# One hybrid layer in f32: where the sums of weight blocks for the up projection are made, and when those for the other products run

## The chip, the cores and the metric

The kernel is one program on one core of a Trainium2 chip. The metric is the device time of one execution in microseconds. A core has TensorE (PE; its weight loads are listed apart as PEld), VectorE (DVE), ScalarE (ACT), GpSimd (POOL) and SyncE (SP), and 16 DMA engines that serve all queues. Here SP issues the loads of weights, and POOL issues small stores and the block sums described below.

## The reference

One layer of a decoder trunk, sequence and width 1024, all of it f32. `u` is the modulated input:

```python
mod = cond @ w_ada[l] + b_ada[l]
shift1, scale1, gate1, shift2, scale2, gate2 = jnp.split(mod[:, None, :], 6, axis=-1)
u = x * (1.0 + scale1) + shift1
hq, hf, hi, hg, rq, rk, rv, rg, ga, gb = jnp.split(u @ w_in[l], split_at, axis=-1)
ya = _hgrn2(hq, hf, hi, hg, lower_bounds[l]) @ w_pa[l]
yb = _retention(rq, rk, rv, rg, positions) @ w_pb[l]
y = (jax.nn.sigmoid(ga) * ya + jax.nn.sigmoid(gb) * yb) @ w_o[l]
x = _layer_norm(DEEPNORM_ALPHA * x + (1.0 + gate1) * y, ln1_g[l], ln1_b[l])
u = x * (1.0 + scale2) + shift2
h = jnp.square(jax.nn.relu(u @ w_up[l] + b_up[l]))
y = h @ w_down[l] + b_down[l]
x = _layer_norm(DEEPNORM_ALPHA * x + (1.0 + gate2) * y, ln2_g[l], ln2_b[l])
```

`w_in` has the columns of HGRN2 (`hq` to `hg`, 8 heads of 128), of retention (`rq` to `rg`, 4 heads) and of the two gates (`ga`, `gb`, 1024 each). `w_pb` is 2048x1024, `w_up` 1024x4096, `w_down` 4096x1024.

## The kernel before

**Products.** Every f32 product is made of three matmuls on halves: `split` writes a rounded copy `hi` (ACT, L181) and the rest `lo` (DVE, L182), and `mm3` multiplies hi by hi, hi by lo and lo by hi (L186 to L188). A `mm3` of 512 columns is three matmuls of 128x512.

**Block products.** The six large products (`gb`, `rg`, `pa`, `pb`, `up`, `dn`) cut both factors into 2x2 blocks and use a scheme of seven block products, q1 to q7, in place of eight. Some take a sum of weight blocks for their weights: with w11, w12, w21, w22 as the blocks, q5 needs s1 = w21 + w22, q6 s2 = s1 + w11, q3 s4 = s2 + w12 and q7 s3 = w11 + w21 (the signs are put into the activations). The activations have such variants too; `t_sums` makes them on DVE, once for each large product.

**The sums.** Each large product is cut into parts (gb 2, rg 4, pa 2, pb 4, up 8, dn 8). `block_sums` makes a part's four sums in DRAM, on POOL's DMA queue: four copies (L207) and four accumulating DMAs (L208) of 512 KB each, 224 DMAs for all 28 parts. `start_sums` puts them in one list behind the start of the program, in the order of the products that need them, and `mm3` takes one from it whenever 14*512 matmul columns have gone by: every fifth `mm3` of 512 columns. `after` ties each to that `mm3`'s last matmul, so that POOL issues it then and not before.

**The stream of weights.** `build_stream` lists every weight tile in the order of use. SP loads pieces of 512 KB into `raw` (three buffers, `_load`), `_split_to` makes `wh` and `wl` of them (three buffers each), two tiles ahead of the product that uses them. Pieces of `w_ada` go through the same `raw` buffers: DVE reads them directly in `ada_step` (L376 and L378, results in `acc`) during retention, four groups of two pieces for each head.

**Order of the program.** The start (to about 60 us); HGRN2, with the projection for `ga` at its end (to about 660); retention, four heads (`r_head`, to 1180; `t` at L762 is the rotation, `gl` and `knl` are halves made by `split`); the gates (`GATE_STEPS`, from 1180); the merge of the branches (to about 1650), the output projection and its norm (`out_proj`, 1650 to 1743; `rs` at L1253 is a row's inverse deviation, made on POOL, `z_d` a store); up (`ffn_up`, 1743 to 2046); down (`ffn_down`, to the end). A scheduler orders each engine's instructions within this.

**Up.** `UP_STEPS` runs q1 and q2 of parts 0 and 1, then q5, q6, q7, q3, q4 of part 0, the same of part 1, and then parts 2 to 7, each in the order q1, q5, q6, q2, q7, q3, q4. A step is 24 matmuls of 128x512. In the first steps DVE and ACT also make the four variants of the activations. `up_block` (L1357 in the trace) writes the squared ReLU into `hv` (two buffers); `part_sums` (L957 to L960) and `last_sum` (L963 to L965) add up its variants for down on DVE and store them to `hv_d` by POOL's queue, one pair of groups after the other. Banks of PE's results are called `psa` to `psd`; `group_out` copies a finished one to `o` (L992).

Of the kernel before, what the change touches and what calls it, by code (L numbers as in the profile page):

```python
# [9 lines left out]
F32 = mybir.dt.float32  # L10
# [4 lines left out]
ALU = mybir.AluOpType  # L15
# [3 lines left out]
P = 128  # L19
# [42 lines left out]
DN_ORDER = ("q1", "q5", "q6", "q3", "q7", "q2", "q4")  # L62
SECOND = ("q2", "q5", "q3")


def group_steps(parts):

    a = parts[:2]
    return ([(q, *x) for q in ("q1", "q2") for x in a] + [(q, *x) for x in a for q in UP_ORDER if q not in ("q1", "q2")] +
            [(q, *x) for x in parts[2:] for q in UP_ORDER])  # L70
# [2 lines left out]
GATE_STEPS = group_steps([("gb", p) for p in range(2)] + [("rg", p) for p in range(4)])  # L73
UP_STEPS = group_steps([("up", p) for p in range(8)])
LAST = 4
PREP = 14 * 512

H_DEFER = (3, 8)
H_ORDER = (("hq", "hf", "hg", "hi"), ("hg", "hi", "hq", "hf"))
# [48 lines left out]
class Rows:  # L128


    def __init__(self, pool):
        self.pool = pool
# [15 lines left out]
class Trunk:  # L148
    def __init__(self, ctx, tc, ins, out):
        self.ctx, self.tc, self.nc, self.i, self.out = ctx, tc, tc.nc, ins, out  # L150
        self.n = 0
        self.pend = []
        self.prep = []
        self.cols_done = 0
        self.paced = False

    def later(self, steps, fn):
        self.pend.append([steps, fn])
# [25 lines left out]
    def mm3(self, out, wh, wl, uh, ul, start, stop, more=False):  # L184
        mm = self.nc.tensor.matmul
        r = mm(out, wh, uh, start=start, stop=False, skip_group_check=more)  # L186
        mm(out, wh, ul, start=False, stop=False, skip_group_check=more)  # L187
        l = mm(out, wl, uh, start=False, stop=stop, skip_group_check=more)  # L188
        self.cols_done += 3 * out.shape[-1]
        if self.paced and self.cols_done >= PREP:  # L190
            self.cols_done = 0
            if self.prep:
                self.after(self.prep.pop(0)(), l)
        return r, l
# [22 lines left out]
            add(3, s4[p], s2[p])  # L217
        return {"q1": w11, "q2": w12, "q3": s4, "q4": w22, "q5": s1, "q6": s2, "q7": s3}

    def start_sums(self):  # L220

        late = lambda n: n // 8 + self.sums[n][0]
        self.prep = [self.sums[n][1] for n in sorted(range(len(self.sums)), key=lambda n: (late(n), n))]
        self.paced = True

    def after(self, a, b):

# [16 lines left out]
    def spec_N(self, w, r0, c0, key):  # L244
# [2 lines left out]
        tiles = [(key + (i,), [((lambda d: d.rearrange("p (k c) -> p k c", k=4)), i, (lambda a: a))]) for i in (0, 1)]  # L247
        return pcs, tiles

    def spec_1(self, ap, key):  # L250
        return [ap], [(key, [((lambda d, a=ap: d if len(a.shape) == 2 else d.rearrange("p (k c) -> p k c", k=a.shape[1])), 0, (lambda a: a))])]

    def build_stream(self, specs):
        self.w_tiles = []
        self.w_pcs = []
        for pcs, tiles in specs:
            base = len(self.w_pcs)
            self.w_pcs += pcs
            for key, ops in tiles:
                self.w_tiles.append((key, [(d, base + i, s) for d, i, s in ops]))  # L260
        self.w_raw = {}
        self.w_dst = {}
        self.w_done = {}
        self.w_next = self.w_split = self.w_load = 0
# [13 lines left out]
    def _split_to(self, n):  # L278
        while self.w_split < min(n, len(self.w_tiles)):
            key, ops = self.w_tiles[self.w_split]  # L280
            self._load_to(max(i for _, i, _ in ops) + 3)
            if key[0] == "ada":
                self.w_done[self.w_split] = [self.w_raw[i] for _, i, _ in ops]
                self.w_split += 1
                continue
            if key[0] == "wo":
                self.split(self.woh[key[1]], self.wol[key[1]], self.w_raw[ops[0][1]])
                self.w_done[self.w_split] = None
                self.w_split += 1
                continue  # L290
            if key in self.w_dst:
                hi, lo = self.w_dst[key]
            else:
                hi = self.wp.tile([P, 1024], F32R, tag="wh", bufs=3, name=self.uid("wh"))
                lo = self.wp.tile([P, 1024], F32R, tag="wl", bufs=3, name=self.uid("wl"))
            for d, i, s in ops:
                self.split(d(hi), d(lo), s(self.w_raw[i]))
            self.w_done[self.w_split] = (hi, lo)
            self.w_split += 1
# [1138 lines left out]
def build(ctx, tc, ins, out):  # L1438
    k = Trunk(ctx, tc, ins, out)
# [25 lines left out]
    specs = []  # L1465
# [6 lines left out]
    for h in range(RH):  # L1472
        specs.append(k.spec_T(w_in, 0, C_RQ + 256 * h, ("rq", h), inter=True))
        specs.append(k.spec_T(w_in, 0, C_RK + 256 * h, ("rk", h), inter=True))
        for b in (0, 1):
            specs.append(k.spec_N(w_in, 0, C_RV + 512 * h + 256 * b, ("rv", h, b)))
            for s, g in ADA_ORDER[4 * h + 2 * b:4 * h + 2 * b + 2]:
                c0 = s * D + 256 * g
                pcs = [ins["w_ada"][512 * i:512 * i + 512, c0:c0 + 256].rearrange("(k p) c -> p k c", p=P) for i in (0, 1)]
# [1 line left out]
    k.sums = []  # L1481
    wv = {}
    for name, w, cut, n in (("gb", w_in[:, C_GB:C_GB + 1024], 1, 2), ("rg", w_in[:, C_RG:C_RG + 2048], 1, 4),
                            ("pa", ins["w_pa"], 0, 2), ("pb", ins["w_pb"], 0, 4),
                            ("up", ins["w_up"], 1, 8), ("dn", ins["w_down"], 0, 8)):
        wv[name] = k.block_sums(name, w, cut, n)
    parts = lambda q, name, p: k.spec_1(wv[name][q][p].rearrange("(k p) c -> p k c", p=P), (q, name, p))
    specs += [parts(*x) for x in GATE_STEPS]
    specs += [parts(q, "pa", p) for q in MERGE_ORDER for p in range(2)]
    for n, (q, p) in enumerate((q, p) for q in MERGE_ORDER for p in range(4)):  # L1490
        specs.append(parts(q, "pb", p))
        if n % 3 == 2 and n // 3 < KT:
            specs.append(k.spec_1(ins["w_o"][n // 3 * P:(n // 3 + 1) * P, :], ("wo", n // 3)))
    specs += [parts(*x) for x in UP_STEPS]
    specs += [parts(q, "dn", p) for q in DN_ORDER for p in range(8)]
    k.build_stream(specs)
    upool, u12pool = ExitStack(), ExitStack()
# [2 lines left out]
    with ExitStack() as s:  # L1500
        k.st = k.pool("start", "right", s)
        k.start()
    k.start_sums()
    k.hst = {}
    k.rot = k.rotary()
    with ExitStack() as s:
# [20 lines left out]
    late, fo = k.gates(rs.close, u12pool.close)  # L1527
# [13 lines left out]
    k.u2f = {}  # L1541
    ops = ExitStack()
    k.op = k.pool("op", "right", ops)
    k.out_proj()

    def close():
# [37 lines left out]
```

## Time and profile before

| | before |
|---|---|
| median of 3 runs (lowest, highest) | 2366.46 us (2359.39, 2379.37) |
| the profiled execution | 2367.19 us, span 2365.4 us |
| granted clock of PE, mean | 0.993 |
| busy: PE, PEld | 2302.0 us (97%), 1970.3 us (83%) |
| busy: DVE, ACT, POOL | 1496.8 us (63%), 911.4 us (39%), 362.8 us (15%) |
| POOL's DMA queue (software) | 213.42 MB, 33.9% of the 16 engines' span |
| SP's DMA queue (hardware) | 245.04 MB, 31.7% |

The span runs from the first to the last recorded instruction; the execution's own time holds a little more. A row of an engine's timeline reads: start, length, engine, line, operation, result <- operands, shape, the number of instructions taken together, and in square brackets the idle time ahead of it with what ended that. A row of the waits reads: who waited <- for whom: total us, how many times, the longest.

### The profile page before, as it was taken

Reading aid. Unit: us, or ns where it says so; the run is one execution under the profiler, and the core shown is the slowest. Engines: PE = TensorE matmul, PEld = TensorE weight load, DVE = VectorE, ACT = ScalarE, POOL = GpSimd, SP = SyncE. Lnnn points to the kernel's source line nnn. Section 1 sums busy time; section 2 is a strip of 40 time slices with the busy share of each in tenths; the row PEclk is TensorE's granted clock in tenths of the full one; section 3 lists DMA queues with packets and bytes.
Section 4 is the critical chain, followed back from the end, with each engine's and each line's share of the span. In section 5 each row is a group of like instructions: output and inputs, shape, how many; then the busy total and the mean of one; then the engine's idle time right before and its main releaser. Section 6 shows DMA issues by size and latency. Waiting matters only on the chain.

```text
span 2365.4 us, 31820 instructions
## 1 busy us (share of the span) xinstructions
PE 2302.0 (97%) x12146; PEld 1970.3 (83%) x12146; DVE 1496.8 (63%) x2684; ACT 911.4 (39%) x1425; POOL 362.8 (15%) x543
## 2 busy tenths in 40 slices
PE   7999999999999999999989999999999999999998
PEld 5888888988779898998978887888888888888886
DVE  7886756577274746556485676667786444544578
ACT  4522222221223232433454444453456555544332
POOL 0222221222312222221232211000000000000000
PEclk9999999999999999999999999999999999999999
DMA  9757565656884967758667867776226464865674
GB/s 268 188 148 163 145 149 152 150 135 161 229 225 107 226 174 175 209 140 228 137 207 246 289 231 277 267 262 231 85 99 218 165 222 161 311 219 190 210 239 155
DMA packets 260361, 460.94 MB, mean 195 GB/s; under 512 B 15488, under 2 KB 158064, under 8 KB 253552
## 3 DMA queue, kind: packets, MB, share of 16 engines
q0 software_dynamic: 65600, 213.42, 33.9%
q1 hardware_dynamic: 194288, 245.04, 31.7%
q8 instruction: 95, 1.56, 0.3%
q14 instruction: 58, 0.48, 0.1%
q10 hardware_dynamic: 320, 0.45, 0.1%
HBM read 380.20 MB, written 196.09 MB: 244 GB/s over the span
## 4 chain that ended last, share of the span: by engine, by line
PE 87%; DVE 7%; DMA 4%; issue 1%; POOL 1%; ACT 1%; ACTq 0%; DVEq 0%; SPq 0%; POOLq 0%
PE psd L188 17%; PE psd L187 17%; PE psd L186 17%; PE psc L186 4%; PE psc L188 4%; PE psc L187 4%; PE psa L188 3%; PE psa L187 3%; PE psa L186 3%; PE psa L590 3%; PE psb L866 3%; DMA raw<-in_w_ada 3%; PE psc L853 2%; PE psb L186 1%; PE psb L187 1%; PE psb L188 1%
## 5 line engine op out<-in xcount | busy, mean ns | idle before, releaser
L182 DVE TENSOR_TENSOR wl<-raw,wh 128x1024 fp32r<-128x1024 f32 (+1 forms) x312 | 328.1, 1057 | 276.4 <-ACT wh L181 272.1
L181 ACT ACTIVATE wh<-raw 128x1024 fp32r<-128x1024 f32 (+1 forms) x312 | 287.8, 929 | 442.0 <-PE psd L187 239.8
L186 PE MATMUL psd<-uh,wh 128*128 128x512 f32 x788 | 315.9, 402 | 0.0
L187 PE MATMUL psd<-ul,wh 128*128 128x512 f32 x788 | 314.2, 399 | 0.4 <-DVE ul L182 0.4
L188 PE MATMUL psd<-uh,wl 128*128 128x512 f32 x788 | 314.2, 399 | 0.0
L186 PE MATMUL psd<-wh,uh 128*128 128x256 f32 x768 | 221.0, 288 | 0.0
L187 PE MATMUL psd<-wl,uh 128*128 128x256 f32 x768 | 218.3, 284 | 0.0
L188 PE MATMUL psd<-wh,ul 128*128 128x256 f32 x768 | 218.1, 284 | 0.0
L182 DVE TENSOR_TENSOR hl<-hr,hh 128x1024 fp32r<-128x1024 f32 x96 | 117.1, 1221 | 132.8 <-ACT hh L181 132.8
L187 PEld LDWEIGHTS psd<-ul,wh 128*128 128x128 f32 x788 | 149.5, 190 | 28.8 <-DVE ul L182 1.2
L188 PEld LDWEIGHTS psd<-uh,wl 128*128 128x128 f32 x788 | 149.4, 190 | 28.5
L186 PEld LDWEIGHTS psd<-uh,wh 128*128 128x128 f32 x788 | 149.1, 190 | 28.3 <-ACT uh L181 0.7
L181 ACT ACTIVATE hh<-hr 128x1024 fp32r<-128x1024 f32 x96 | 101.4, 1056 | 178.9 <-PE psb L187 68.1
L186 PEld LDWEIGHTS psd<-wh,uh 128*128 128x128 f32 x768 | 147.0, 191 | 2.9 <-issue 2.6
L187 PEld LDWEIGHTS psd<-wl,uh 128*128 128x128 f32 x768 | 147.0, 191 | 0.4
L188 PEld LDWEIGHTS psd<-wh,ul 128*128 128x128 f32 x768 | 147.1, 191 | 0.0
L597 DVE COPY_PREDICATED hS<-mask,psa 128x128 f32<-128x128 uint8 x288 | 77.2, 314 | 28.5 <-PE psa L590 25.9
L823 DVE SCALAR_TENSOR_TENSOR vl<-psd,cst,vh 128x256 fp32r<-128x256 f32 x64 | 30.8, 482 | 76.0 <-ACT vh L822 76.0
L822 ACT ACTIVATE vh<-psd,cst 128x256 fp32r<-128x256 f32 x64 | 30.3, 474 | 117.0 <-PE psd L188 114.6
L590 PE MATMUL psa<-qp,k 128*128 128x192 f32 x384 | 72.6, 329 | 1.3 <-DVE k L566 1.3
L590 PEld LDWEIGHTS psa<-qp,k 128*128 128x128 f32 x384 | 62.1, 189 | 10.4 <-issue 5.0
L1253 POOL TENSOR_TENSOR rs<-rs,mhalf 128x1 f32<-128x1 f32 x16 | 12.0, 747 | 369.9 <-DVE rs L1252 340.5
(503 smaller groups left out, 5687.2 us busy)
## 6 DMA issues: line engine op xcount, KB each, us to landing
raw<-in_w_in SPq DMA_DIRECT2D x90, 512.0 KB, 5.2
hr<-hv_d SPq DMA_DIRECT2D x56, 512.0 KB, 3.5
up_s<-in_w_up POOLq DMA_DIRECT2D x48, 512.0 KB, 5.8
dn_s<-in_w_down POOLq DMA_DIRECT2D x48, 512.0 KB, 5.4
hv_d<-hv POOLq DMA_DIRECT2D x16, 1280.0 KB, 5.8
raw<-in_w_ada SPq DMA_DIRECT2D x32, 512.0 KB, 6.5
raw<-up_s SPq DMA_DIRECT2D x32, 512.0 KB, 6.0
raw<-dn_s SPq DMA_DIRECT2D x32, 512.0 KB, 4.4
```

What stands on the lines that cost most here:

```text
L181: self.nc.scalar.activation(hi, src, AF.Copy)
L182: self.nc.vector.tensor_tensor(lo, src, hi.bitcast(F32), op=ALU.subtract)
L186: r = mm(out, wh, uh, start=start, stop=False, skip_group_check=more)
L187: mm(out, wh, ul, start=False, stop=False, skip_group_check=more)
L188: l = mm(out, wl, uh, start=False, stop=stop, skip_group_check=more)
L590: nc.tensor.matmul(pa[:, c * 192:(c + 1) * 192].rearrange("p (b w r) -> p b w r", w=2, r=3 * sz), k[:, n * P:(n + 1) * P], mv, start=True, ...
L597: V.copy_predicated(dst, self.mask8[:, o:o + 128].rearrange("p (b two s) -> p b two s", two=2, s=sz), src)
L822: nc.scalar.activation(hi, pd, AF.Copy, scale=sc)
L823: nc.vector.scalar_tensor_tensor(lo, pd, sc, hi.bitcast(F32), op0=ALU.mult, op1=ALU.subtract)
L853: mm(G[e], l[:, n % 2, es], r, start=n == 0 and i == 0, stop=i == 2, skip_group_check=n > 0)
L866: mm(po, l, r, start=i == 0, stop=i == len(pairs) - 1)
L1253: nc.gpsimd.tensor_tensor(rs, rs, self.mhalf[:, :1], op=ALU.pow)
```

## The change

Three things change.

1. Up's 64 sums in DRAM go. Its stream holds the blocks of `w_up` themselves (`spec_sums`), and `sum_split` adds them in SBUF on DVE just ahead of the split. q5 loads w21 and w22 and writes their sum into two new tiles `ws` of 128x512; q6 adds w11 to them, and q2's block w12 is added behind its own split, so that q3 finds its weights in `ws`. Parts 0 and 1 run q2 first, so there q3 loads w12 again. q7 loads w11 and w21 and adds them in place. q5, q6 and q3 are split in halves.
2. The rest of the list is cut in two. The 96 sums of `gb`, `rg`, `pa` and `pb` start behind the start as before; the 64 of `dn` start at the output projection.
3. `PREP` goes from 14*512 to 17*512: one sum for every sixth `mm3` of 512 columns in place of every fifth.

```diff
+BLOCKS_OF = {"q1": [(0, 0)], "q2": [(0, 1)], "q3": [], "q4": [(1, 1)], "q5": [(1, 0), (1, 1)], "q6": [(0, 0)], "q7": [(0, 0), (1, 0)]}
...
-PREP = 14 * 512
+PREP = 17 * 512
...
-        if self.paced and self.cols_done >= PREP:
+        if self.cols_done >= PREP:
...
-    def start_sums(self):
-
-        late = lambda n: n // 8 + self.sums[n][0]
-        self.prep = [self.sums[n][1] for n in sorted(range(len(self.sums)), key=lambda n: (late(n), n))]
-        self.paced = True
+    def start_sums(self, n):
+
+        now, self.sums = self.sums[:n], self.sums[n:]
+        late = lambda n: n // 8 + now[n][0]
+        self.prep += [now[n][1] for n in sorted(range(len(now)), key=lambda n: (late(n), n))]
+        self.cols_done = 0
...
+    def spec_sums(self, w, steps):
+
+        kh, nh = w.shape[0] // 2, w.shape[1] // 2
+        specs, seen = [], set()
+        for q, name, p in steps:
+            late = q == "q3" and (name, p, "q2", "early") in seen
+            if q == "q2" and (name, p, "q6") not in seen:
+                seen.add((name, p, "q2", "early"))
+            seen.add((name, p, q))
+            need = [(0, 1)] if late else BLOCKS_OF[q]
+            pcs = [w[kh * k:kh * k + kh, nh * m + 256 * p:nh * m + 256 * p + 256].rearrange("(k p) c -> p k c", p=P) for m, k in need]
+            specs.append((pcs, [((q, name, p), [(None, i, late) for i in range(len(pcs))])]))
+        return specs
+
+    def sum_split(self, q, hi, lo, raws, late):
+
+        V = self.nc.vector
+        hi, lo = (x.rearrange("p (k c) -> p k c", k=4) for x in (hi, lo))
+        if q in ("q5", "q6", "q3"):
+            if q == "q5":
+                self.ws = [self.gp.tile([P, 2, 256], F32, tag="gate", bufs=2, name=self.uid("ws")) for _ in (0, 1)]
+            for k, s in zip((slice(0, 2), slice(2, 4)), self.ws):
+                if q == "q5":
+                    V.tensor_tensor(s, raws[0][:, k], raws[1][:, k], op=ALU.add)
+                elif q == "q6" or late:
+                    V.tensor_tensor(s, s, raws[0][:, k], op=ALU.add)
+                self.split(hi[:, k], lo[:, k], s)
+            return
+        if q == "q7":
+            V.tensor_tensor(raws[0], raws[0], raws[1], op=ALU.add)
+        self.split(hi, lo, raws[0])
+        if q == "q2" and self.ws_open:
+            for k, s in zip((slice(0, 2), slice(2, 4)), self.ws):
+                V.tensor_tensor(s, s, raws[0][:, k], op=ALU.add)
...
-                            ("pa", ins["w_pa"], 0, 2), ("pb", ins["w_pb"], 0, 4),
-                            ("up", ins["w_up"], 1, 8), ("dn", ins["w_down"], 0, 8)):
+                            ("pa", ins["w_pa"], 0, 2), ("pb", ins["w_pb"], 0, 4), ("dn", ins["w_down"], 0, 8)):
...
-    specs += [parts(*x) for x in UP_STEPS]
+    specs += k.spec_sums(ins["w_up"], UP_STEPS)
...
-    k.start_sums()
+    k.start_sums(96)
...
+    assert not k.prep
+    k.start_sums(64)
     k.out_proj()
```

**POOL's queue in retention.** Before, the list runs through retention; `small` (L883) is a head norm's inverse deviation, and the DMAs between are copies for up's sums:

```order
L883 TENSOR_TENSOR small_6836<-small_6836,mhalf 128x1
L207 DMA up_s_6_185<-in_w_up 512x256
L883 TENSOR_TENSOR small_6897<-small_6897,mhalf 128x1
L883 TENSOR_TENSOR small_6977<-small_6977,mhalf 128x1
L207 DMA up_s_6_193<-in_w_up 512x256
L883 TENSOR_TENSOR small_7038<-small_7038,mhalf 128x1
L207 DMA up_s_6_201<-in_w_up 512x256
L883 TENSOR_TENSOR small_7114<-small_7114,mhalf 128x1
L207 DMA up_s_6_209<-in_w_up 512x256
```

In the changed kernel the last sums of the first list (`pb`) stand among the last stores of `ga`, which end HGRN2, and the first norms of retention (now L928) follow with no sum between them:

```order
L719 DMA ga_d_87<-gate_5699 128x512
L209 DMA pb_s_3_170<-pb_s_3_166 64x2048
L209 DMA pb_s_3_178<-pb_s_3_170 64x2048
L719 DMA ga_d_87<-gate_5729 128x512
L719 DMA ga_d_88<-gate_5763 128x512
L719 DMA ga_d_88<-gate_5791 128x512
L958 DMA g_d_130<-brow_6543 16x1x16
L958 DMA g_d_130<-brow_6658 16x1x16
L928 TENSOR_TENSOR small_6760<-small_6760,mhalf 128x1
L928 TENSOR_TENSOR small_6820<-small_6820,mhalf 128x1
```

The sums have left retention's rows of POOL; the norms follow one another there.

**POOL's queue at the end of the output projection and in up.** Before, the stores of `hv_d` for the first pair of groups come right behind the projection's own work:

```order
L1253 TENSOR_TENSOR rs_15957<-rs_15957,mhalf 128x1
L1339 DMA z_d_112<-rows1l 128x1024
L960 DMA hv_d_119<-hv_16291 128x2560
L960 DMA hv_d_119<-hv_16309 128x2560
L965 DMA hv_d_119<-hv_16291 128x1024
L965 DMA hv_d_119<-hv_16309 128x1024
```

In the changed kernel down's sums (copies L208, accumulating DMAs L209) stand around the same stores (now L1005 and L1010):

```order
L208 DMA dn_s_4_183<-in_w_down 256x512
L208 DMA dn_s_4_191<-in_w_down 256x512
L208 DMA dn_s_4_199<-in_w_down 256x512
L208 DMA dn_s_4_207<-in_w_down 256x512
L1005 DMA hv_d_119<-hv_16180 128x2560
L1005 DMA hv_d_119<-hv_16198 128x2560
L1010 DMA hv_d_119<-hv_16180 128x1024
L1010 DMA hv_d_119<-hv_16198 128x1024
L209 DMA dn_s_2_205<-dn_s_2_189 64x2048
L209 DMA dn_s_3_190<-dn_s_3_182 64x2048
```

Each sum waits for its `mm3`, and a store behind it in the queue waits with it.

**ACT's queue where part 0 of up hands over to part 1.** Before, the first two writes of `hv` (L1357) stand ahead of the copies of the banks `psd` and `psb` (L992):

```order
L992 ACTIVATE o_16417<-psc_16404 128x512
L181 ACTIVATE wh_16436<-raw_16358 128x1024
L992 ACTIVATE o_16432<-psc_16419 128x512
L1357 ACTIVATE hv_16487<-o_16102 128x512
L992 ACTIVATE o_16452<-psd_16029 128x512
L1357 ACTIVATE hv_16505<-o_16104 128x512
L181 ACTIVATE wh_16470<-raw_16398 128x1024
L992 ACTIVATE o_16466<-psb_16042 128x512
```

In the changed kernel (L1037 and L1402 for the same lines) both copies come ahead of both writes of `hv`, and the splits of `ws` come in halves:

```order
L1037 ACTIVATE o_16325<-psc_16311 128x512
L1037 ACTIVATE o_16340<-psc_16327 128x512
L182 ACTIVATE wh_16306<-raw_16205 128x1024
L182 ACTIVATE wh_16344<-ws_16209 128x512
L182 ACTIVATE wh_16344<-ws_16210 128x512
L1037 ACTIVATE o_16365<-psd_15891 128x512
L182 ACTIVATE wh_16384<-raw_16304 128x1024
L1037 ACTIVATE o_16380<-psb_15905 128x512
L1402 ACTIVATE hv_16401<-o_15966 128x512
L1402 ACTIVATE hv_16420<-o_15968 128x512
```

What moved are the `hv` writes, from between the two copies to behind both.

More of the change, by code (lines that the diff above doesn't have):

```diff
@@ L154, in __init__ @@
         self.cols_done = 0
-        self.paced = False
     def later(self, steps, fn):
@@ L260, in build_stream @@
                 self.w_tiles.append((key, [(d, base + i, s) for d, i, s in ops]))
+        self.ws_open = False
         self.w_raw = {}
@@ L280, in _split_to @@
             key, ops = self.w_tiles[self.w_split]
-            self._load_to(max(i for _, i, _ in ops) + 3)
+            if ops:
+                self._load_to(max(i for _, i, _ in ops) + 3)
             if key[0] == "ada":
@@ L295, in _split_to @@
                 lo = self.wp.tile([P, 1024], F32R, tag="wl", bufs=3, name=self.uid("wl"))
+            if key[1] == "up":
+                q = key[0]
+                late = q == "q3" and bool(ops)
+                self.ws_open = q == "q6" or self.ws_open and q != "q3"
+                self.sum_split(q, hi, lo, [self.w_raw[i] for _, i, _ in ops], late)
+                ops = []
             for d, i, s in ops:
```

## The prediction

> **What bounds the kernel now.** I read the head of the page and its chain first, then the stretches by stage, then who TensorE (PE) waited for, and last the DMA lines.
>
> ```profile
> span 2365.4 us, 31820 instructions
> PE 87%; DVE 7%; DMA 4%; issue 1%; POOL 1%; ACT 1%; ACTq 0%; DVEq 0%; SPq 0%; POOLq 0%
> ```
>
> The chain that ended last runs through PE for 87% of the span. The matmuls are the same before and after, so only two things can move the end: gaps in PE, and the clock at which PE runs behind a gap. The stretches show where gaps are (columns: length, then busy time of PE, PEld, DVE, ACT, POOL, then PEclk, DMA share, GB/s):
>
> ```profile
> 40.00:660.00 620.00, 606.58 (x3367) 523.16 (x3366) 417.49 (x1045) 178.31 (x338) 140.55 (x188) 0.99 0.66 164
> 660.00:1180.00 520.00, 505.23 (x3516) 467.33 (x3514) 305.93 (x640) 173.55 (x364) 118.07 (x167) 0.99 0.71 181
> 1180.00:1240.00 60.00, 53.50 (x236) 43.01 (x236) 47.95 (x50) 30.43 (x41) 18.12 (x32) 0.94 0.58 199
> 1640.00:1743.00 103.00, 101.94 (x477) 84.59 (x476) 76.34 (x113) 39.26 (x67) 7.95 (x14) 1.00 0.28 101
> 1743.00:2046.00 303.00, 300.91 (x1330) 248.04 (x1329) 159.77 (x186) 178.77 (x254) 15.95 (x30) 1.00 0.56 192
> ```
>
> HGRN2 (40 to 660) loses 13.4 us of PE, retention (660 to 1180) 14.8, the head of the gates (1180 to 1240) 6.5, the output projection 1.1 and the up projection 2.1. The gates' 6.5 us stand behind vector sums of activations, which the change leaves alone. Retention is the stage that it empties of sums; what PE and VectorE (DVE) waited for there:
>
> ```profile
> PE psa L776 <- DVE t L762: 9.0, 3, 5.0
> PE psc L853 <- DVE gl L182: 4.3, 1, 4.3
> PE psa L186 <- DVE knl L182: 1.0, 2, 0.6
> DVE acc L378 <- DMA raw<-in_w_ada: 19.6, 7, 6.5
> DVE acc L376 <- DMA raw<-in_w_ada: 6.7, 4, 3.1
> ```
>
> PE waits for DVE, and DVE for the `w_ada` pieces that the ada groups read (26.3 us over 11 waits). The longest case, from the chain and from DVE's and POOL's order of time:
>
> ```profile
> 929.47 10.50 DMA raw<-in_w_ada
> 932.55 1.00 DVE L378 SCALAR_TENSOR_TENSOR acc<-raw,cond,acc 128x256 f32<-128x256 f32 x2
> 940.07 2.05 DVE L378 SCALAR_TENSOR_TENSOR acc<-raw,cond,acc 128x256 f32<-128x256 f32 x4 [6.52 <-DMA raw<-in_w_ada]
> 928.12 0.79 POOL L208 DMA_DIRECT2D dn_s<-dn_s  x1 [2.57 <-PE psd L188]
> 931.52 0.88 POOL L208 DMA_DIRECT2D dn_s<-in_w_down  x1 [2.61 <-PE psd L188]
> 693.10 9.05 DMA raw<-in_w_ada
> 696.16 1.53 DVE L378 SCALAR_TENSOR_TENSOR acc<-raw,cond,acc 128x256 f32<-128x256 f32 x3
> ```
>
> DVE takes its queue in order, so while it waits at 933.55 for a piece that needed 10.5 us, the rotation (`t`) that PE wants stands behind it. During those 10.5 us POOL issued accumulating sums, 3.40 us apart.
>
> **The change part by part.**
>
> *Sums leave retention.* When do they run?
>
> ```profile
> L207 POOL DMA_DIRECT2D up_s<-in_w_up x32: 623/640/712, 512.2 to 798.3; - x32
> L208 POOL DMA_DIRECT2D dn_s<-dn_s x16: 789/824/911, 895.3 to 1166.0; - x16
> raw<-in_w_ada SPq DMA_DIRECT2D x9, 512.0 KB, 7.4
> raw<-in_w_up SPq DMA_DIRECT2D x6, 512.0 KB, 3.8
> ```
>
> Before, up's and down's 128 sums lie from 512 to 1166 us, all through retention. After, only gates and branches (96 sums) run in front, one per 6 products instead of 5, that is every 4.08 us at best instead of 3.40. Before, they filled the time to about 512; in the new order the last of them stands among the last `ga` stores, at the end of HGRN2, so retention has none. The third row is a `w_ada` piece between 920 and 1060, beside sums: 7.4 us. The fourth is a piece of equal size and 1 KB rows between 1745 and 1850, without sums: 3.8 us. I take 3.8 (bounds 3.8 and 7.4). Then the piece of 929.47 lands at 933.3, before DVE is through at 933.55; that of 693.10 at 696.9, before 697.69. Both waits vanish. What is late next there is DVE's own split of `knl`, 1.0 us in two waits, and 0.2 us of issue, which I leave in. Of 14.5 us waited, 13.3 go.
>
> Each long gap is followed by a slow stretch:
>
> ```profile
> 707.00:710.00 3.00, 2.94 (x14) 2.94 (x15) 1.95 (x6) 0.96 (x3) 0.00 (x0) 0.51 0.41 138
> 943.90:947.00 3.10, 3.03 (x11) 2.73 (x12) 2.69 (x6) 2.43 (x4) 0.00 (x0) 0.50 0.36 121
> 947.00:950.00 3.00, 3.00 (x16) 2.55 (x14) 2.86 (x7) 0.00 (x0) 0.59 (x1) 0.69 0.11 26
> 1078.07 0.41 PE L776 MATMUL psa<-cst,t 128*128 128x128 f32 x2 [2.89 <-DVE t L762]
> 1078.00:1082.00 4.00, 3.93 (x14) 3.35 (x15) 1.61 (x4) 2.38 (x4) 0.00 (x0) 0.57 0.60 213
> ```
>
> At granted clocks of 0.51, 0.50, 0.69 and 0.57 they lose 1.5 + 1.6 + 0.9 + 1.7 = 5.7 us, which go with the gaps. Retention: −13.3 − 5.7 = **−19.0 us** (bounds 0 and −20.2).
>
> The gap ahead of the fourth stretch was 2.89 us long, and the clock fell to 0.57 behind it. The Trainium skill, page "TensorE: Matmul & The Clock Gate", Part 1, has the clock fall only after an idle window of about 3.4 us; by it that gap would have no slow stretch, and the term would be 1.7 us smaller. The measured 0.57 decides.
>
> *HGRN2's sums run slower.* They load the DMA queues less, but DVE's and PE's orders also shift by some instructions between about 110 and 200 us, where this stall stands:
>
> ```profile
> 135.52 0.89 PE L554 MATMUL psa<-q,k 128*128 128x192 f32 x4 [2.88 <-DVE hS L558]
> ```
>
> A stall of 2.9 us with a slow stretch like that of the 2.89 us one above (1.7) is 4.6 us, which may go or come again once. I take 0 (bounds −4.6 and +4.6).
>
> *64 sums in the output projection and up.* Pacing restarts at the projection's first matmuls, so 64 × 4.08 = 261 us from about 1650 to 1915. They sit in POOL's queue among `rs` (the row's inverse deviation), whose slack I read here:
>
> ```profile
> 1665.12 0.56 POOL L1253 TENSOR_TENSOR rs<-rs,mhalf 128x1 f32<-128x1 f32 x1 [35.49 <-DVE rs L1252]
> 1671.60 0.87 PE psa L1331 x8
> ```
>
> The first `rs` stands behind three sums, the third due 12.2 us after 1650; DVE delivers at 1665.1. A sum that comes late could hold it up to 4.08 us, and PE wants the result only at 1671.6, 6.5 us later. Cost 0 (bounds 0 and +2).
>
> *Up's weights are added in SBUF.* Per part: six adds of 128x512 and one of 128x1024, and three splits cut in halves.
>
> ```profile
> L182 DVE TENSOR_TENSOR wl<-raw,wh 128x1024 fp32r<-128x1024 f32 x55 | 67.3, 1223 | 91.2 <-ACT wh L181 91.2
> L958 DVE TENSOR_TENSOR hv<-hv 128x512 f32<-128x512 f32 x14 | 9.6, 685 | 0.0
> L181 ACT ACTIVATE wh<-raw 128x1024 fp32r<-128x1024 f32 x55 | 58.5, 1063 | 59.8 <-PE psd L187 34.9 <-PE psc L187 17.8 <-PE psb L187 5.1
> ```
>
> DVE: 48 × 0.685 + 8 × 1.22 + 24 × (2 × 0.685 − 1.223) = 32.9 + 9.8 + 3.5 = 46.2 us, all beside matmuls: its 159.8 busy us of 303 become 206. It also idles 91.2 us ahead of splits, waiting for ScalarE (ACT), which waits for PE to free a `wh` buffer; that idle time hides the adds. Without this cover the 46.2 us would be on the path. ACT's 24 extra halves cost under 24 × 1.06 = 25 us of its 124 idle. SP issues 66 loads where it issued 56; with three raw buffers a piece is asked for when the third one ahead of it has been split, two steps of 24 matmuls (24 × 0.227, a fifteenth of the 3.40 us pace, is 5.4 us) before its own split: 10.9 us of room for 3.8 to 7.4.
>
> The tight place is the head, where four variants of the activations are made as well, and the hand-over from part 0 to part 1:
>
> ```profile
> 1767.84 0.50 PE L188 MATMUL psd<-q6h,wl 128*128 128x512 f32 x1 [0.40 <-DVE wl L182]
> 1803.44 0.63 ACT L1357 ACTIVATE hv<-o 128x512 f32<-128x512 f32 x1 [2.19 <-DMA hv_d<-hv]
> 1807.53 0.63 ACT L1357 ACTIVATE hv<-o 128x512 f32<-128x512 f32 x1 [2.98 <-DMA hv_d<-hv]
> 1809.65 0.50 PE L186 MATMUL psb<-q7h,wh 128*128 128x512 f32 x1 [1.59 <-ACT o L992]
> ```
>
> At 1803 ACT waits for `hv`'s store, behind it stands the copy of the bank `psb`, and PE loses 1.59 us. In the new order that copy comes ahead of both `hv` writes: −1.6. At the head I followed DVE's new queue with the durations above: the split for q6 is complete some 0.7 us later than now, the one for q7 before PE reaches it, that for q3 0 to 1 us late. With the store of `hv` waiting on POOL behind paced sums, I take +2 for all of up's new stalls (bounds 0 and +12, the latter one wait of 4.08 us at each of the pairs 1 to 3).
>
> **Sum.** The profiled execution took 2367.19 us, 1.8 more than its span and 0.7 more than the median of 2366.46. 2367.2 − 19.0 + 0 + 0 − 1.6 + 2.0 = 2348.6; less the 0.7, **2348 us**.
>
> **The rivals.**
>
> *A, the pieces stay late.* In retention `w_ada` pieces come four in a row through three raw buffers, so part of the 7.4 us may be their own queue. Against it: the same queue landed at 3.8 in up. Retention then gives nothing: 2367.2 − 1.6 + 2 − 0.7 = 2367.
>
> *B, up gives part of it back.* POOL's queue is in order:
>
> ```profile
> 1790.91 0.53 POOL L960 DMA_DIRECT2D hv_d<-hv  x1 [39.31 <-DVE hv L957]
> 1797.58 0.53 POOL L965 DMA_DIRECT2D hv_d<-hv  x1 [1.09 <-DVE hv L963]
> ```
>
> The stores went out as soon as DVE had them; now two to four sums, each paced, stand between them. Should PE wait 4.08 us at each of pairs 1 to 3, 12 us come back: 2359. For it speaks that ACT already waits here; against it that from pair 2 on `hv` is first written four steps (21.7 us) after the last product of the pair before.
>
> The Trainium skill, page "SBUF — State Buffer", the box on DVE blocking software DMA, speaks against more SBUF-to-SBUF vector work beside POOL's DMAs, since POOL cannot write descriptors while certain DVE instructions hold a shared port; were it so here, each sum would hold POOL longer and B would be likelier than A. The row of `up_s` says otherwise: between 623 and 712 ns for all 32, at a DVE 59% busy (305.93 of 520). B keeps its chance.
>
> *C, slower.* Beside the sums, up's raw pieces land later than their 10.9 us of room, because four bursts meet: sums, `hv` stores and the double loads of q5 and q7. From there each late piece is a PE gap. At 16 us, 5 us late plus 1.7 of slow clock, twice in each of the four and a half parts that overlap the sums: 9 × 6.7 = 60 us, so 2348.6 − 2 + 60 − 0.7 = 2406. It decides from 10.9 us; the longest landing quoted above is 10.5, while a median of 3.8 or 7.4 is far from it.
>
> **How the numbers follow.** Forecast 0.66 (own range 2337 to 2356, from the bounds of HGRN2 and of up), A 0.11, B 0.16, C 0.07. The range 2337 to 2364 holds the forecast, B and a weak A. A measurement of this kernel tells about 1% (24 us) from no change. Faster by over 1% needs less than 2342.8: the forecast's lower quarter with HGRN2 on the good side, 0.18. Slower by over 1%: C, 0.06 of it. The rest, 0.76, lies within.
>
> **What would show it.** Retention some 19 us shorter, without a gap of PE over 1 us; `w_ada` landing near 4 us; no clock of 0.5 between 660 and 1180. `dn_s` rows from about 1650 to 1915. DVE near 206 us in up, ACT waiting for `hv_d` without PE waiting for ACT. I am wrong if `w_ada` still needs 7 us without sums, or if PE in up waits for `wl` or `wh` by more than 5 us in all.

## The result and the profile after

The changed kernel takes 2388.76 us (median of 8 runs, 2384.67 to 2392.37) against 2367.2 us for the kernel before on the same chip: a ratio of 1.0089, 95% interval 1.0069 to 1.0109. It is slower by 21.6 us, where 2348 us was forecast and 2364 us was the end of the range.

The head of the page and its chain, then the stretches that were shown of before (columns as there):

```profile
span 2386.3 us, 31820 instructions
PE 81%; DMA 7%; DVE 7%; issue 3%; ACT 1%; POOL 1%; ACTq 0%; DVEq 0%; SPq 0%; POOLq 0%
PE psd L187 16%; PE psd L188 16%; PE psd L189 16%; DMA raw<-in_w_up 4%; PE psc L187 3%; PE psc L188 3%; PE psc L189 3%; PE psa L635 3%; PE psb L911 3%; PE psa L189 3%; PE psa L188 3%; PE psa L187 3%; PE psc L898 2%; DVE wl L183 1%; PE psb L187 1%
40.00:660.00 620.00, 600.60 (x3343) 518.58 (x3342) 414.88 (x1039) 178.72 (x337) 118.98 (x160) 0.99 0.56 142
660.00:1180.00 520.00, 518.57 (x3612) 479.79 (x3611) 319.61 (x656) 183.60 (x381) 46.82 (x73) 1.00 0.26 84
1640.00:1743.00 103.00, 102.82 (x486) 85.52 (x485) 76.53 (x113) 46.29 (x85) 25.47 (x40) 1.00 0.77 212
1743.00:2046.00 303.00, 278.45 (x1177) 226.27 (x1176) 177.99 (x241) 156.41 (x240) 44.43 (x68) 0.95 0.85 260
```

Retention runs at 518.57 of 520 us, its clock at 1.00 and the DMA share down from 0.71 to 0.26. Up has lost what was won there: PE idles 24.6 of 303 us, the clock is 0.95, and `raw<-in_w_up` has come into the chain with 4% of the span.

The stages are measured between four rows of PE that both traces have (before first, then after): the last `ob` of HGRN2, the second variant `q6l` in the gates, the first `woh` of the output projection, and the hand-over in up (before, this last one is the prediction's row of 1809.65).

```profile
607.50 0.63 PE L649 MATMUL psb<-cst,ob 128*128 128x128 f32 x4 [1.53 <-DVE ob L641]
1202.61 0.73 PE L187 MATMUL psd<-q6l,wh 128*128 128x512 f32 x2 [1.50 <-DVE q6l L182]
1649.59 0.47 PE L186 MATMUL psd<-woh,yh 128*128 128x512 f32 x1 [1.06 <-DVE y L1145]
```
```profile
613.26 0.63 PE L694 MATMUL psb<-cst,ob 128*128 128x128 f32 x4 [1.20 <-DVE ob L686]
1188.12 0.73 PE L188 MATMUL psd<-q6l,wh 128*128 128x512 f32 x2 [1.50 <-DVE q6l L183]
1634.88 0.47 PE L187 MATMUL psd<-woh,yh 128*128 128x512 f32 x1 [1.39 <-DVE y L1190]
1809.59 0.80 PE L187 MATMUL psb<-q7h,wh 128*128 128x512 f32 x1 [12.10 <-ACT o L1037]
```

HGRN2 ends 613.26 − 607.50 = 5.8 us later. From there to the gates it takes 574.9 in place of 595.1 us: −20.3. The gates and the merge are even (446.8 and 447.0). From `woh` to the end of the span it takes 751.4 in place of 715.8 us: +35.6, of which 14.7 have gathered by the hand-over (174.7 against 160.1 from `woh`). The sum is 5.8 − 20.3 − 0.2 + 35.6 = 20.9 us, the difference of the spans. Up itself explains the 35.6: PE idles 22.5 us more in it than before, and a clock of 0.95 over 278.45 busy us costs an estimated 14 us.

The waits in up say through whom it came:

```profile
ACT wh L182 <- DMA raw<-in_w_up: 33.2, 5, 13.8
DVE ws L275 <- DMA raw<-in_w_up: 29.7, 7, 7.1
PE psb L187 <- ACT o L1037: 12.1, 1, 12.1
PE psd L187 <- DVE o L1043: 8.6, 3, 3.4
```

PE hardly waits for the weights themselves (0.9 us for `wl` and 0.6 for `wh`). It waits for copies and adds of its own banks (`o`) that stand in ACT's and DVE's queues behind work that waits for a late piece. The worst case, from the chain, and the queues of POOL and ACT at that place:

```profile
1790.31 1.22 DVE raw L281
...
1791.55 16.36 DMA raw<-in_w_up
1807.99 1.06 ACT wh L182
```
```profile
1788.53 0.54 POOL L1005 DMA_DIRECT2D hv_d<-hv  x1 [1.25 <-ACT o L1037]
1790.08 1.14 POOL L1010 DMA_DIRECT2D hv_d<-hv  x2 [1.01 <-DVE hv L1008]
1791.20 1.70 POOL L209 DMA_DIRECT2D dn_s<-dn_s  x2
1795.06 0.89 POOL L209 DMA_DIRECT2D dn_s<-in_w_down  x1 [2.16 <-PE psb L189]
1793.56 0.58 ACT L1037 ACTIVATE o<-psd 128x512 f32<-128x512 f32 x1
1807.99 1.06 ACT L182 ACTIVATE wh<-raw 128x1024 fp32r<-128x1024 f32 x1 [13.85 <-DMA raw<-in_w_up]
1808.95 0.58 ACT L1037 ACTIVATE o<-psb 128x512 f32<-128x512 f32 x1
```

The piece can only be asked for at 1791.55, when DVE's add for q7 has freed a buffer. Around it POOL issues the stores of `hv` and three accumulating sums, and the piece needs 16.36 us. While it was under way the 16 DMA engines were busy throughout (a share of 1.03 by the profile); before, between 1780 and 1800 with the same stores and no sums, it was 0.65. ACT came to its split at 1794.1, and the copy of `psb` behind the split comes at 1808.95; PE has waited 12.1 us.

### The profile page after: what moved, and what is told of

Read it like the earlier page. It is cut to its first block, busy times and chain, and to the rows that moved or that the text cites. A ratio compares the mean times of both kernels' runs of the same rounds, so it can differ in the third digit from the quotient of the medians.

```text
span 2386.3 us, 31820 instructions
## 1 busy us (share of the span) xinstructions
PE 2306.3 (97%) x12146; PEld 1971.8 (83%) x12146; DVE 1535.2 (64%) x2764; ACT 913.0 (38%) x1451; POOL 313.3 (13%) x479
## 4 chain that ended last, share of the span: by engine, by line
PE 81%; DMA 7%; DVE 7%; issue 3%; ACT 1%; POOL 1%; ACTq 0%; DVEq 0%; SPq 0%; POOLq 0%
PE psd L187 16%; PE psd L188 16%; PE psd L189 16%; DMA raw<-in_w_up 4%; PE psc L187 3%; PE psc L188 3%; PE psc L189 3%; PE psa L635 3%; PE psb L911 3%; PE psa L189 3%; PE psa L188 3%; PE psa L187 3%; PE psc L898 2%; DVE wl L183 1%; PE psb L187 1%
## 5 line engine op out<-in xcount | busy, mean ns | idle before, releaser
L183 DVE TENSOR_TENSOR wl<-raw,wh 128x1024 fp32r<-128x1024 f32 (+1 forms) x288 | 298.7, 1043 | 230.8 <-ACT wh L182 226.1
L182 ACT ACTIVATE wh<-raw 128x1024 fp32r<-128x1024 f32 (+1 forms) x288 | 262.3, 917 | 441.1 <-PE psd L188 210.3
L187 PE MATMUL psd<-wh,hh 128*128 128x512 f32 x168 | 65.5, 390 | 0.9 <-ACT o L1401 0.9
```

Of the source, the lines that this page charges most:

```text
L182: self.nc.scalar.activation(hi, src, AF.Copy)
L183: self.nc.vector.tensor_tensor(lo, src, hi.bitcast(F32), op=ALU.subtract)
```

## The experiments

Times are medians against the kernel before, run beside on the same chip; the last two columns are taken as above from the one profile of each (`ob` to `q6l`, and `woh` to the end of the span; before has 595.1 and 715.8). The last column of the e3 run, which leaves up as it was, reads 720.4, so differences of 5 us in it are not resolved.

| run | what it is | us, before | ratio (95%) | retention | projection to end |
|---|---|---|---|---|---|
| changed | the change | 2388.76, 2367.2 | 1.0089 (1.0069–1.0109) | 574.9 | 751.4 |
| e1 | dn sums in front, adds in up | 2370.6, 2366.29 | 1.0016 (0.9999–1.0034) | 583.5 | 723.3 |
| e2 | sums beside up, no adds | 2369.3, 2366.29 | 1.0001 (0.9982–1.0021) | 586.0 | 727.5 |
| e3 | before, PREP 17 | 2406.02, 2366.29 | 1.0155 (1.0118–1.0192) | – | 720.4 |
| e4 | changed, PREP 14 | 2383.15, 2366.29 | 1.0068 (1.0051–1.0086) | 575.0 | 753.9 |
| e5 | e1 with PREP 12 | 2378.77, 2367.9 | 1.0042 (1.0022–1.0062) | 589.1 | 723.5 |
| e6 | changed, one more buffer | 2401.5, 2367.9 | 1.0144 (1.0113–1.0174) | 575.5 | 764.1 |
| e7 | e1 with PREP 14 | 2365.18, 2367.9 | 0.9990 (0.9977–1.0003) | 590.1 | 721.0 |
| e8 | changed, one load a step | 2397.19, 2367.9 | 1.0125 (1.0101–1.0149) | 574.8 | 763.4 |
| e9 | 124 sums in front, 36 late, PREP 14 | 2356.6, 2367.37 | 0.9953 (0.9938–0.9968) | 574.7 | 730.5 |
| e10 | changed, rotary stores by SP | 2385.28, 2367.37 | 1.0071 (1.0054–1.0087) | 574.7 | 753.5 |
| e11 | changed, no adds | 2358.53, 2367.37 | 0.9959 (0.9946–0.9973) | 574.6 | 725.2 |
| e12 | e9 with 130 and 30 | 2359.45, 2366.96 | 0.9967 (0.9952–0.9983) | 578.0 | 726.2 |

### Which half of the change loses it: e1 and e2

```diff
# e1
-    k.start_sums(96)
+    k.start_sums(160)
...
-    k.start_sums(64)
# e2: up back in block_sums and in the stream as before, and
-    k.start_sums(96)
+    k.start_sums(160)
```

> The changed kernel with down's 64 sums back in front (160 sums in one list from the start, one per 6 products), so that none runs beside up; up's weights are still added in SBUF. Theory S (the sums beside up make the raw pieces late): up's pieces land in 4 to 7 us as they did once the sums had ended, PE idles under 5 us in up, and of the 35 us that up and down lost some 30 come back; retention has sums again until about 1000 us, so only its last gap (some 5 us) stays away: 2362 to 2372 us. Rival D (two loads for q5 and q7 through three raw buffers are late by themselves): PE still idles about 25 us in up, 2390 to 2405 us.

> The changed kernel with up's sums made in DRAM again (160 sums in front: gates, branches, up; one per 6 products) and down's 64 still beside the output projection and up. Theory S: pieces of up land at 10 us and more beside the sums, although each step has one load only; PE idles over 10 us in up and the time is 2380 to 2400 us. Rival D: with one load a step nothing is late, PE idles under 5 us in up and the time is 2362 to 2370 us. In between, both are needed.

Neither half alone loses much. From the projection to the end, adds without sums cost 723.3 − 715.8 = 7.5 us and sums without adds 11.7 us, together 19.2; the two at once cost 35.6, more than the sum by over three times what this measure resolves. e1 came as theory S had it (2370.6 us, 4.9 us of idle PE in up), so D alone is refuted. e2 took 2369.3 us where S had 2380 and more, so S alone is refuted too, although its pieces are late and PE idles 9.5 us in up. The landings of the pieces between 1780 and 1940 us (all of `raw`; least, median, most), first e1, then e2:

```profile
DMA to landing us min/median/max: 3.8/5.0/9.3
```
```profile
DMA to landing us min/median/max: 4.3/8.7/18.5
ACT wh L182 <- DMA raw<-in_w_up: 19.0, 6, 5.4
ACT wh L182 <- DMA raw<-up_s: 14.2, 4, 8.0
PE psd L187 <- ACT o L1401: 5.3, 2, 3.3
```

The sums make pieces late (18.5 us against 9.3 at most). In e2 they are as late as in the changed kernel (16.4 at most), and ACT waits the same 33.2 us for them, yet PE waits 9.4 us in all (the largest group is shown) against 24.4 in the changed kernel.

### What makes a late piece dear: e6, e8 and e11

```diff
# e6, in _load: the second block of q5 and q7
+        if i in self.w_second and self.xp:
+            t = self.xp.tile([P, 1024], F32, tag="rawx", bufs=1, name=self.uid("rawx"))
# e8
-"q5": [(1, 0), (1, 1)], ... "q7": [(0, 0), (1, 0)]
+"q5": [(1, 0)], ... "q7": [(0, 0)]
-                    V.tensor_tensor(s, raws[0][:, k], raws[1][:, k], op=ALU.add)
+                    V.tensor_tensor(s, raws[0][:, k], raws[-1][:, k], op=ALU.add)
# e11: one block a step for q3, q5, q6, q7 as well, and in place of sum_split
+                self.split(hi, lo, self.w_raw[ops[0][1]]...)
```

> The changed kernel with one more load buffer in up: the second block of q5 and of q7 goes to a tile of its own (4 KB a partition, the most that fits there) in place of one of the three raw buffers. The bytes, the sums beside up and DVE's adds stay. Theory R (room: q5 and q7 hold two of three raw buffers until DVE's add, so the next pieces are asked for too late; a landing of 16 us then stops ACT's queue): PE idles under 12 us in up in place of 26 and the time is 2362 to 2373 us. Rival B (the DMA engines are full, the pieces would be late whenever they are asked for): 2380 to 2390 us.

> The changed kernel with the second block of q5 and of q7 left out: the first is added to itself, so up's result is another one. 16 loads of 512 KB fewer in up, one buffer a step; DVE's adds, the split halves and the sums beside up stay. Theories R and B both: up loses 5 to 12 us in place of 35, 2360 to 2370 us. Rival A (the adds and halves in DVE's and ACT's queues make up's loss): 2380 us and more.

> The changed kernel with the adds of up's blocks left out: q5, q6, q3 and q7 each load one block of w_up and split it, so up's result is another one. 56 loads as before the change, none of them double; down's sums stay beside up. Theory Q (a late piece costs PE little while only a split on ACT waits for it; it costs PE much where an add on DVE waits for it, since the copies and adds of PE's banks stand behind it in DVE's queue): up loses about 12 us as with up's sums in DRAM, retention stays empty of sums: 2355 to 2366 us, with pieces still landing at 14 to 20 us. Rival: the late pieces cost PE the same wherever they are waited for: 2380 to 2395 us.

e6 and e8 came out slower than the changed kernel: e6 outside both of its forecasts, e8 where rival A had it. Neither the missing buffer nor the second loads are the whole cause. What the free buffer was to bring did come: neither run has the wait of 12.1 us at the hand-over. But PE waits behind DVE instead, in e6 as follows:

```profile
PE psc L189 <- DVE wl L183: 19.8, 3, 8.0
PE psd L187 <- DVE o L1049: 10.4, 1, 10.4
```

e8 has 50 loads and keeps the adds; it needs 763.4 us from the projection to the end. e11 has 56 loads, one a step, and no adds: 725.2. Both have sums beside up and late pieces. Those of e11 land as in the changed kernel (there 7.1 us in the median and 16.4 at most), those of e8 later (the waits of up and the landings, first e8, then e11):

```profile
DMA to landing us min/median/max: 3.8/14.5/21.9
DVE ws L275 <- DMA raw<-in_w_up: 62.4, 5, 17.5
PE psc L189 <- DVE wl L183: 21.3, 4, 7.3
PE psd L187 <- DVE o L1043: 8.4, 1, 8.4
```
```profile
DMA to landing us min/median/max: 4.0/8.0/18.5
ACT wh L182 <- DMA raw<-in_w_up: 31.6, 11, 7.9
PE psd L187 <- ACT o L1404: 3.6, 2, 2.6
```

In e11 ACT waits 31.6 us for pieces and PE 7.6 us in all (3.0 at the hand-over), against 24.4 in the changed kernel with pieces as late; in e8 DVE waits 62.4 us for the blocks of q5 alone and PE some 30 behind it. The queue of DVE in e8 shows why:

```profile
1815.10 1.29 DVE L275 TENSOR_TENSOR ws<-raw 128x512 f32<-128x512 f32 x2 [15.21 <-DMA raw<-in_w_up]
1816.31 0.68 DVE L1043 TENSOR_TENSOR o<-o,psd 128x512 f32<-128x512 f32 x1
1816.91 0.68 DVE L1043 TENSOR_TENSOR o<-o,psb 128x512 f32<-128x512 f32 x1
```

The add for the next part's q5 stands ahead of the adds of PE's banks `psd` and `psb`. It waits 15.2 us for its piece, and they wait with it. So the changed kernel loses in two ways: 12.1 us where two loads hold the buffers and the next piece is asked for late, and most of the rest behind adds that wait in DVE's queue. e11 has neither. That the scheduler set the add earlier in e6 and e8 than in the changed kernel, because their pieces are asked for earlier in the program, would explain why these lose more; that was not tried by itself.

### HGRN2's 5.8 us: e3, e4 and e10

```diff
# e3: the kernel before with PREP = 17 * 512; e4: the changed kernel with PREP = 14 * 512
# e10
-            nc.gpsimd.dma_start(self.sin_d[:, cs], n)
+            nc.sync.dma_start(self.sin_d[:, cs], n)
# and cos_d likewise
```

> The kernel before with PREP alone at 17*512. Theory P (the new pace sets HGRN2's stall, since it moves accumulating sums onto the rotary table's stores, for which DVE waits): the PE gap near 140 us is about 7 us long in place of 2.9 and HGRN2 ends some 6 us later, 2368 to 2374 us. Rival: the stall comes from the other parts of the change; then it stays at 2.9 us and the time within 3 us of before.

> The changed kernel with PREP back at 14*512. Theory P: the PE gap near 140 us is back at about 2.9 us and HGRN2 ends 4 to 6 us earlier. Beside up the sums now come every 3.40 us and end near 1870 in place of 1943 us: by theory S fewer parts of up are late but those more, and the time is 2378 to 2392 us. Rival D: up's loss does not depend on the sums' pace, 2382 to 2386 us, with late pieces in the parts without sums as well.

> The changed kernel with the stores of the rotary tables (sin_d, cos_d) issued by SP in place of POOL, so that they don't stand among the paced sums. Theory P (these stores make HGRN2's stall, since DVE waits for their landing before it writes the same tiles again): DVE's wait of 4.1 us near 131 us falls under 2 us and PE's gap near 141 us from 7.0 to 3 us or less; the rest as in the changed kernel: 2380 to 2386 us. Rival: the stall comes from DVE's load of work at that place, whatever the store; then the gap stays at 6 to 7 us and the time at 2386 to 2391 us.

PE's stall in HGRN2, `psa` waiting for the state `hS` that DVE writes, was 2.88 us before and 6.97 in the changed kernel; it is 6.33 in e3 and 3.04 in e4, which ends HGRN2 8.1 us sooner than the changed kernel (its last `ob` is at 605.18). The pace alone moves the stall. The end of HGRN2 scatters as well: in e6, e8 and e11, whose edits touch up alone, the stall is 6.0 to 6.9 us and the last `ob` stands at 609.11, 611.09 and 610.94. So the 5.8 us of the one profile after are 1.6 to 5.8 with these three. The rows in front of it, of the changed kernel and then of e4:

```profile
122.95 1.09 POOL L209 DMA_DIRECT2D gb_s<-in_w_in  x1
124.17 1.06 POOL L782 DMA_DIRECT2D cos_d<-rot  x1
125.48 1.08 POOL L209 DMA_DIRECT2D gb_s<-in_w_in  x1 [0.25 <-PE psd L189]
131.19 0.29 DVE L769 TENSOR_SCALAR rot<-rot 128x256 f32<-128x256 f32 x1 [4.10 <-DMA cos_d<-rot]
141.04 1.62 PE L599 MATMUL psa<-q,k 128*128 128x192 f32 x4 [6.97 <-DVE hS L603]
```
```profile
120.62 0.29 DVE L749 TENSOR_SCALAR rot<-rot 128x256 f32<-128x256 f32 x1 [1.76 <-DMA sin_d<-rot]
122.73 0.30 DVE L769 TENSOR_SCALAR rot<-rot 128x256 f32<-128x256 f32 x1 [0.58 <-DMA cos_d<-rot]
133.05 1.62 PE L599 MATMUL psa<-q,k 128*128 128x192 f32 x4 [3.04 <-DVE hS L603]
```

The rotary tables are made in two tiles that are written again once their stores have landed. At the new pace a store falls between two accumulating sums, DVE waits for it, and the writes of `hS` stand behind. In e10, with the stores on SP, the sums still run beside them: DVE's wait falls to 3.02 and the stall to 4.94, half of the way to e4 and not to the 3 us expected. So POOL's order is part of it; the traffic of the accumulating sums may be the other, which no run shows by itself. For up e4 decides nothing: its 2383.15 us lie in both of its forecasts.

e3 held a surprise: 2406 us. At the slower pace the sums no longer end in retention; the last is issued at 1370.90, in the gates, where small stalls add up (PE is busy for 189.3 of the 220 us from 1180 to 1400, before for 213.5). From `ob` to `woh` it takes 1076 us in place of 1042.

### Versions: e5, e7, e9 and e12

```diff
# e5, e7: e1 with PREP = 12 * 512 and 14 * 512
# e9: the changed kernel with
-PREP = 17 * 512
+PREP = 14 * 512
-    k.start_sums(96)
+    k.start_sums(124)
-    k.start_sums(64)
+    k.start_sums(36)
# e12: 130 and 30
```

> The changed kernel with all 160 sums in front and PREP 12*512 (one sum every four products), so that they end at about 660 us, ahead of retention: no sums in retention nor up. If the gains add up: retention at 519 us of PE in 520 with no gap over 1.5 us, up with a loss of about 7 us as with down's sums in front at every sixth product, and HGRN2's stall near 138 us between 2.9 and 7 us: 2350 to 2362 us. Rival H: the denser sums make HGRN2's own pieces and stores late; it ends 10 us or more later and the time is 2365 to 2385 us.

> The changed kernel with all 160 sums in front and PREP 14*512 (every five products). HGRN2's stall near 135 us at about 3 us as in the two kernels with that pace (4 to 6 us sooner than with every sixth), sums in retention until about 850 us: the gap near 705 us stays, those near 943 and 1078 us do not come; up loses about 7 us: 2357 to 2366 us. Rival: the stall in HGRN2 does not go with the pace but with the order, then 2364 to 2372 us.

> The changed kernel with PREP 14*512, 124 of the 160 sums in front (done before retention) and 36 from the output projection on (done before the first stores of hv in up). Up's weights are added in SBUF as in the changed kernel. Theories S and Q: HGRN2's stall near 2.5 to 3 us, no gap over 1.5 us in retention, late pieces nowhere, PE idle under 6 us in up: 2345 to 2355 us. Rival D (up's adds cost as such): PE idles 10 us and more in up although no sum runs beside it, 2358 us and more.

> The version with 124 and 36 sums, with 130 in front and 30 from the output projection on. There the sums still met the head of up: DVE waited 6.7 us for a piece at 1740 us with the activations' variants behind it, PE 4.75 us at 1749, and a slow stretch followed. Six sums fewer end some 20 us sooner, ahead of these loads. Theory Q: the wait at 1740 us falls under 3 us and PE's gap there under 2 us, 2349 to 2354 us, against 2356.6. Rival: the six sums at the front run into retention and cost as much there, or up's head waits without sums too: 2355 to 2360 us.

e9 is faster than both kernels: 2356.6 us, 0.5% below before. It keeps retention free (574.7) and HGRN2's stall at 2.47 us; what it misses of its forecast (PE idles 9.5 us in up, under 6 were expected) is a wait at the head of up, the same mechanism, since its late sums reach into it. e12 has six sums fewer there and was to mend that; its 2359.45 us lie where its rival had them, for the six sums run into retention (the last is issued at 682.60, and the stage takes 578.0 us), and the stall at the head of up merely moved:

```profile
1738.39 0.69 DVE L275 TENSOR_TENSOR ws<-raw,raw 128x512 f32<-128x512 f32 x1 [7.32 <-DMA raw<-in_w_up]
1741.40 0.50 PE L189 MATMUL psc<-u2h,wl 128*128 128x512 f32 x1 [4.25 <-DVE wl L183]
```

That piece was asked for at 1726.6 among accumulating sums that were still being issued and took 11.67 us. e5 puts all sums ahead of retention at one per four products. Then HGRN2's stall is 11.24 us, and the last sums, issued until 693 us, meet retention's first `w_ada` pieces: DVE waits 12.5 us and PE 11.3. Its 2378.77 us are rival H's: denser is no way out. e7, with one per five products, is even with before: its 2365.18 us lie in both of its forecasts, and the stall of 2.5 us in HGRN2 speaks for the pace. With sums in retention until 836.53 us it wins 5.0 us there and loses 5.2 from the projection on.

## Why the prediction was wrong

**Retention was right.** −19.0 us was forecast, −20.3 measured, with the mechanism as described. The landings of `w_ada` between 660 and 1180 us, before and after:

```profile
DMA to landing us min/median/max: 3.4/5.5/10.5
```
```profile
DMA to landing us min/median/max: 3.4/3.6/5.4
  DMA raw<-in_w_ada: 1.4, 1
```

The 26.3 us over 11 waits are 1.4 over one, and no clock of 0.5 is left there. Rival A is refuted. The table bears it out: every version without sums after 660 us needs 574.6 to 575.5 us for the stage, e12 with its six 578.0, and those with more 583.5 to 595.1.

**The output projection was right:** 0 forecast, and 102.82 of 103 us measured, with sums in it.

**HGRN2 was mis-sized.** 0 with bounds of ±4.6 was taken; +5.8 came in the one profile after, and +1.6 to +3.6 in e6, e8 and e11. The bound counted the stall as one that goes or comes again once. It hangs on a wait for a store, which goes with the sums around it, and was 2.3 to 11.2 us long in the runs here (in the changed kernel 4.1 us longer than before; the other 1.7 us are within the scatter of these ends). The rows of DVE ahead of the stall would have shown the store of `rot`; only the shift of the order was weighed.

**The failing step is up: "10.9 us of room for 3.8 to 7.4".** Both numbers were wrong. The room was worked out as if each step needed one piece, but q5 and q7 hold two of the three buffers until DVE's add; the piece of 1791.55 had 2.6 us until ACT came to it. And 7.4 us was a median: beside sums and the stores of `hv` a piece took up to 16.4, with the DMA share at 1.03. The stores are not needed for that: in e9 pieces asked for one close behind the other between 1730 and 1734 took up to 21.4 us beside sums, and its first store of `hv` is issued at 1782.43. The up stage, with the hand-over, was put at −1.6 + 2.0 = +0.4 us, and projection, up and down came to +35.6. The sign that was named for this, PE waiting over 5 us for `wl` or `wh`, did not come (1.5 us): the wait took another way.

**The hand-over** was to give 1.6 us, since the copy of `psb` went ahead of the writes of `hv`. It did go ahead of them, but a split that waits for a late piece stands ahead of the copy, and 1.59 became 12.1. Even without sums beside up, in e1, that split waits 6.3 us for its piece and PE 3.1, so the term was wrong in its sign and not only beside the sums.

**Rival C had the place and the cause, at 0.07.** It named the bursts (sums, `hv` stores, double loads) and put the time at 2406; 2389 was measured. It was dismissed by the longest landing quoted, 10.5 us, which came from another stage. It also expected PE to wait for the weights; in fact the wait reaches PE through DVE's and ACT's queues. That is why "the idle time hides the adds" failed as well: the adds fit into DVE's idle time by their length (it is busy for 178.0 of 303 us), but they wait for DMA and block the queue. Rival B, a wait for `hv`'s store, plays a small part: no PE wait in up is put down to it.

**Two sums of the prediction don't come out.** The forecast's own range, 2337 to 2356, does not follow from the bounds named: ±4.6 for HGRN2 and 0 to +12 for up in place of +2 give 2341 to 2363 about 2348. Rival B's 12 us in place of up's +2 give 2358, not 2359. Neither would have held 2389.

On the rule from the Trainium skill, "SBUF — State Buffer", box on DVE blocking software DMA: the box speaks of certain operations of DVE, with an fp32 copy as its example, while up's adds are `TENSOR_TENSOR`. The two accumulating sums at 1791.20 take 0.85 us each to issue while DVE adds `ws` (1791.44 to 1792.72); before, in retention, one took 0.88. So no run here shows POOL's descriptors held up by the added DVE work.

## What to carry to other kernels

Adding an operation to an engine's queue is not priced by its length against that engine's idle time, but by what it waits for and what stands behind it: an add that reads a DMA's landing is a possible stop for every later instruction of that engine. A load's landing time has to be read where the new load will run, beside the transfers that will run there, and its room counted from the moment a buffer is really free, with all buffers that the step holds. When two edits are made at once, try each alone: here each alone came within 5 us of before, and the pair cost some 18 us more.

## What was not expected of the hardware

A 512 KB piece that took 3.8 us without sums took up to 16.4 us beside the sums and stores of the changed kernel, 21.4 us beside sums in e9 and 21.9 us in e8, although the sums themselves come only one in 3.4 or 4.1 us at best. Before the change, with the same stores of `hv` and no sums, `raw` landed between 1780 and 1940 us as follows:

```profile
DMA to landing us min/median/max: 3.7/3.8/9.0
```
